# A mixture-of-experts stage on one core: second biases for all tokens at once, tokens gathered one expert ahead at set places, 15 instead of 17 ranks with split operands

## The chip, the cores and the metric

One Trainium2 chip, one of its cores. The metric is the device time of one launch in microseconds. TensorE (PE) multiplies into PSUM; VectorE (DVE), ScalarE (ACT) and GpSimd (POOL) do the rest; SyncE (SP) issues the weight transfers from DRAM.

## The reference

Three transformer blocks over 512 tokens of width 1024, in float32. The change touches the mixture of experts at the end of the first block:

```python
top_val, top_idx = lax.top_k(logits, TOP_K)          # 4 of 32 experts per token
gates = jax.nn.softmax(top_val, axis=-1)
u = xb @ w1[e] + b1[e]                               # 1024 -> 2048
glu = jnp.minimum(u[:, ::2], SWIGLU_LIMIT)
lin = jnp.clip(u[:, 1::2], -SWIGLU_LIMIT, SWIGLU_LIMIT)
a = glu * jax.nn.sigmoid(SWIGLU_ALPHA * glu) * (lin + 1.0)
y_e = a @ w2[e] + b2[e]                              # 1024 -> 1024
y = sum over the token's experts of gate * y_e
x = x + gt_f * y
```

Each expert has 12.6 MB of weights, and each is read once.

## The kernel before

The stage is `moe(k)` (line 951 on). A router ranks experts 1 to 31 by their number of tokens; expert 0 has rank 0 whatever its count. `ROOM` gives each rank its rows: 128, 96, 80 or 64. Tokens beyond a rank's room go to overflow blocks, which a loop at the end runs (none does here). Ranks 1 and 2 ("heavy") have a second block of 64 rows beside their 128.

An expert is three products ("gemms") of 8 contraction steps `kt` each, with 1024 output columns per step: two for the halves of the first layer, one for the second layer. A rank below `N1` ("large") runs on split operands: each weight unit of 128x1024 is copied rounded by ACT (`whi`, L302) and its remainder taken by DVE (`wlo`, L303), and each step is three products of two 512-column matmuls. A rank from `N1` up ("small", 64 rows) multiplies the raw float32 weights instead; the two column halves go to two halves of the array and no splitting is needed. Heavies do both.

Each gemm opens with a bias matmul (`bias` times a selector, L1306 for small, L1309 for large) and the weights follow (L1321). After either half of the first layer DVE and ACT form the gated activation (`gl`, L1338 to L1342), PE transposes it (`to_features`, L1252), and `put` (L1244, L1246) writes it as the operand `a`. After the third gemm ACT scales the rows by their gates (`yr`) and GpSimd adds them into a DRAM array by an indirect DMA (`scatter`). The tokens of an expert come by an indirect DMA from `hrow` (`gather`, L1275 for small, L1279 for large) into one of two tiles `xg`, are transposed and put as operand `x`.

The weights stream through a ring of nine 1 MB tiles `mraw` and two `raw`, issued by SP in one order. `Stream.ahead` starts splits up to three units ahead. The order of experts is written out by a planner: it alternates large and small by a budget and puts a heavy where the budget is low. With `N1 = 17` it gives 0, 3, 17, 4, 5, 18, 6, 7, 19, 8, 9, 20, 10, 11, 21, 12, 13, 22, 14, 15, 23, 16, 24, 1, 25, 26, 27, 2, 28, 29, 30, 31; with `N1 = 15` it gives 0, 3, 15, 4, 5, 16, 6, 7, 17, 8, 9, 18, 10, 11, 19, 12, 13, 20, 14, 21, 1, 22, 23, 24, 2, 25, 26, 27, 28, 29, 30, 31. The framework orders each engine's instructions by program order and by its own estimate of when their inputs are ready, within the edges it is given; `issue_after(ins)` is such an edge: instructions of the block stand behind `ins` on its engine. The tables of tokens and gates are formed during expert 0 (`tables`, `tables2`). For the last expert `collect()` takes two `mraw` tiles to read the DRAM sums back, and `first_weights` loads weights of the second block.

## Time and profile before

| | us |
|---|---|
| median of 3 runs | 3357.71 (3354.88 to 3361.1) |
| the profiled execution, its own time | 3355.98 |
| its span, first to last instruction | 3354.2 |
| busy PE / DVE / ACT / POOL in the span | 3210.9 / 1920.1 / 1337.2 / 411.0 |
| stage of the experts, first gemm of rank 0 to first gemm of rank 31 | 706.6 to 1819.6 |

Busy time of PE is the union of its matmuls, which overlap. In the trace a float32 matmul has two records. The stage's stretches are cut at the first bias matmul of each expert, which the timeline of PE shows. A profile row's last bracket names the idle time before an instruction and what ended it. In rows of stretches the columns are the stretch, its length, busy time (and number) on PE, PEld, DVE, ACT and POOL, the granted clock, the DMA engines' busy share and GB/s.

### The profile page before, as it was taken

Reading aid. Unit: us, or ns where it says so; the run is one execution under the profiler, and the core shown is the slowest. Engines: PE = TensorE matmul, PEld = TensorE weight load, DVE = VectorE, ACT = ScalarE, POOL = GpSimd, SP = SyncE. Lnnn points to the kernel's source line nnn. Section 1 sums busy time; section 2 is a strip of 40 time slices with the busy share of each in tenths; the row PEclk is TensorE's granted clock in tenths of the full one; section 3 lists DMA queues with packets and bytes.
Section 4 is the critical chain, followed back from the end, with each engine's and each line's share of the span. In section 5 each row is a group of like instructions: output and inputs, shape, how many; then the busy total and the mean of one; then the engine's idle time right before and its main releaser. Section 6 shows DMA issues by size and latency. Waiting matters only on the chain. (4 is left out here: it accounts for less than half of the span.)

```text
span 3354.2 us, 41112 instructions
## 1 busy us (share of the span) xinstructions
PE 3210.9 (96%) x15657; PEld 2236.1 (67%) x15657; DVE 1920.1 (57%) x2931; ACT 1337.2 (40%) x1972; POOL 411.0 (12%) x514
## 2 busy tenths in 40 slices
PE   6999999999999999999997899999999999999998
PEld 5778887776665555544342567777776777678876
DVE  7652235476786666844141477756547756555645
ACT  2233344345565555633131254322235433343433
POOL 1223000131000000000100100312120011110001
PEclk9999999999999999999999999999999999999999
DMA  7437313459999999996979312545332200022222
GB/s 268 170 119 237 111 71 115 184 200 354 393 393 380 378 374 371 378 387 239 407 298 367 139 59 75 191 155 187 132 116 75 98 25 3 30 85 96 93 91 85
DMA packets 110393, 664.75 MB, mean 198 GB/s; under 512 B 15452, under 2 KB 15556, under 8 KB 41712
## 3 DMA queue, kind: packets, MB, share of 16 engines
q1 hardware_dynamic: 81952, 573.35, 44.2%
q0 software_dynamic: 28240, 88.73, 8.9%
q8 instruction: 125, 2.05, 0.2%
q14 instruction: 76, 0.62, 0.1%
HBM read 647.04 MB, written 28.10 MB: 201 GB/s over the span
## 5 line engine op out<-in xcount | busy, mean ns | idle before, releaser
L302 ACT ACTIVATE whi<-raw 128x1024 fp32r<-128x1024 f32 x354 | 373.7, 1058 | 661.2 <-PE mm L353 512.3
L303 DVE TENSOR_TENSOR wlo<-raw,whi 128x1024 fp32r<-128x1024 f32 x352 | 434.5, 1238 | 311.7 <-ACT whi L302 304.9
L352 PE MATMUL mm<-h_hi,whi 128*128 128x512 f32 x1440 | 578.0, 401 | 4.7 <-DVE th L656 1.6
L353 PE MATMUL mm<-h_lo,whi 128*128 128x512 f32 x1440 | 577.5, 401 | 0.0
L354 PE MATMUL mm<-h_hi,wlo 128*128 128x512 f32 x1440 | 576.6, 400 | 0.0
L303 DVE TENSOR_TENSOR wlo<-mraw,whi 128x1024 fp32r<-128x1024 f32 x246 | 294.4, 1219 | 73.5 <-ACT whi L302 73.0
L352 PEld LDWEIGHTS mm<-h_hi,whi 128*128 128x128 f32 x1440 | 271.3, 188 | 83.0 <-issue 11.5
L353 PEld LDWEIGHTS mm<-h_lo,whi 128*128 128x128 f32 x1440 | 271.5, 189 | 68.2 <-issue 7.0
L354 PEld LDWEIGHTS mm<-h_hi,wlo 128*128 128x128 f32 x1440 | 271.5, 189 | 67.8 <-issue 5.6
L302 ACT ACTIVATE whi<-mraw 128x1024 fp32r<-128x1024 f32 x248 | 258.2, 1055 | 84.6 <-PE mm L1321 62.7
L1321 PE MATMUL s<-mraw,x 128*64 128x512 f32 x896 | 235.4, 605 | 23.9 <-DMA mraw<-in_w_dram 15.5
L1321 PE MATMUL mm<-whi,x 128*80 128x512 f32 (+2 forms) x816 | 242.4, 403 | 6.7 <-ACT whi L302 6.7
L1338 DVE TENSOR_SCALAR gl<-s 128x256 f32<-128x256 f32 x34 | 14.4, 423 | 309.4 <-PE s L1321 309.4
L1321 PEld LDWEIGHTS mm<-whi,x 128*80 128x80 f32 (+2 forms) x816 | 134.6, 168 | 76.2 <-issue 13.5
L1321 PEld LDWEIGHTS s<-mraw,x 128*64 128x64 f32 x896 | 65.7, 138 | 146.4 <-issue 123.3
L370 PE MATMUL mm<-whi,h_hi 128*128 128x256 f32 x480 | 138.3, 288 | 2.8 <-DVE rs L620 1.7
L352 PE MATMUL mm<-fhi,whi 128*128 128x512 f32 x352 | 139.2, 396 | 0.0
L353 PE MATMUL mm<-flo,whi 128*128 128x512 f32 x352 | 139.0, 395 | 0.0
L354 PE MATMUL mm<-fhi,wlo 128*128 128x512 f32 x352 | 138.9, 395 | 0.0
L1339 ACT ACTIVATE gt<-gl 128x256 f32<-128x256 f32 (+3 forms) x68 | 35.5, 522 | 257.7 <-DVE gl L1338 256.2
L371 PE MATMUL mm<-wlo,h_hi 128*128 128x256 f32 x480 | 136.4, 284 | 1.8 <-DVE wlo L303 1.7
L1321 PE MATMUL mm<-wlo,x 128*80 128x512 f32 (+2 forms) x408 | 131.7, 404 | 5.6 <-DVE wlo L303 4.3
(731 smaller groups left out, 5560.3 us busy)
## 6 DMA issues: line engine op xcount, KB each, us to landing
mraw<-in_w_dram SPq DMA_DIRECT2D x316, 1024.0 KB, 8.9
raw<-in_w_dram SPq DMA_DIRECT2D x68, 1024.0 KB, 9.7
mw<-in_wmod_dram POOLq DMA_DIRECT2D x48, 512.0 KB, 4.2
raw<-in_w_dn_dram SPq DMA_DIRECT2D x24, 1024.0 KB, 4.8
raw<-in_w_gu_dram SPq DMA_DIRECT2D x22, 1024.0 KB, 4.9
raw<-in_w_up_dram SPq DMA_DIRECT2D x22, 1024.0 KB, 4.8
mw<-in_wada_dram POOLq DMA_DIRECT2D x32, 512.0 KB, 4.4
raw<-in_w_aqk_dram SPq DMA_DIRECT2D x12, 1024.0 KB, 4.8
```

The lines of the kernel that those rows point to most:

```text
L302: nc.scalar.activation(hi, raw, AF.Copy)
L303: ins = (nc.gpsimd if pool_lo else nc.vector).tensor_sub(lo, raw, hi.bitcast(F32))
L352: nc.tensor.matmul(pss[t], hi[:, k, s], xs[0][:, k0 + k], start=first, stop=False)
L353: nc.tensor.matmul(pss[t], hi[:, k, s], xs[1][:, k0 + k], start=False, stop=False)
L354: nc.tensor.matmul(pss[t], lo[:, k, s], xs[0][:, k0 + k], start=False, stop=last)
L370: nc.tensor.matmul(ps, xs[0][:, k, s], hi[:, k % 4], start=k == 0, stop=False)
L371: nc.tensor.matmul(ps, xs[0][:, k, s], lo[:, k % 4], start=False, stop=False)
L1321: ins = nc.tensor.matmul(o[c], l(kt), r_[:, c * 512:(c + 1) * 512], start=False, stop=kt == 7 and n_ == len(terms) - 1)
L1338: V.tensor_scalar(gl, pg, 7.0, None, op0=ALU.min)
L1339: S.activation(th, gl, AF.Tanh, scale=0.5 * 1.702)
```

## The change

`N1` goes from 17 to 15, and `ROOM` gives ranks 15 and 16 64 rows. `gemm` leaves the bias matmul out of the third gemm. In its place `tables2` forms `gT`, the gate of each token for each expert (one product and one sum on DVE, a copy on ACT, four transposes, a copy on ACT), and `bias2(n)` adds, for eight feature tiles, second bias times `gT` to `x` (one float32 matmul of 512 columns, one DVE instruction); the eight are handed to rank 30 (`order[-2]`), two per step in the second half of its first gemm. `gather` returns its transposes as steps; `expert` gathers for the expert that follows it and places the steps with `issue_after` behind steps 3 and 5 of its second gemm, or behind steps 3 to 5 of the third when either is heavy, or behind 5 and 6 of the third in expert 0. The transposes of the activation are placed behind step 2 of the next gemm. `sw` (the selector) is copied by ACT, not GpSimd. The five units whose remainder GpSimd took in expert 0 (6, 10, 12, 14, 19) go to DVE.

```diff
--- before.py
+++ after.py
@@ -942,9 +942,9 @@
     k.wcol = None
 
 
-N1 = 17
+N1 = 15
 N2 = 2
-ROOM = (128,) * 6 + (96,) * 4 + (80,) * 7 + (64,) * 15
+ROOM = (128,) * 6 + (96,) * 4 + (80,) * 5 + (64,) * 17
 OV = 32 + N2
 NB = OV + 15
 
@@ -1181,6 +1181,16 @@
         V.tensor_copy(ovi, ov[0:1])
         V.tensor_tensor(sel[:, :, 32:47], ov[:, 1:16].unsqueeze(1).to_broadcast([128, 2, 15]),
                         pmod.unsqueeze(2).to_broadcast([128, 2, 15]), op=ALU.is_equal)
+
+        V.tensor_tensor(big.rearrange("p (t r) e -> p t r e", t=4), E, gate.unsqueeze(3).to_broadcast([128, 4, 4, 32]), op=ALU.mult)
+        gr = e2[:, 0:128].rearrange("p (t e) -> p t e", t=4)
+        V.tensor_reduce(gr, big.rearrange("p (t r) e -> p t e r", t=4), axis=AX.X, op=ALU.add)
+        g4 = e1[:, 512:1024].rearrange("p (t a e) -> p t a e", t=4, a=4)
+        S.activation(g4, gr.unsqueeze(2).to_broadcast([128, 4, 4, 32]), AF.Copy)
+        ps = k.pt("t")
+        for t in range(4):
+            nc.tensor.transpose(ps[:, t * 128:(t + 1) * 128], g4[:, t].rearrange("p a e -> p (a e)"), k.ident)
+        S.activation(gT, ps, AF.Copy)
         g = k.v("g_final")
         g2 = ep.tile([128, 8], F32, name="g2", bufs=1)
         V.tensor_mul(g2, g, g)
@@ -1189,6 +1199,7 @@
         pools["Y"] = es.enter_context(tc.tile_pool(name="Yp", bufs=1))
 
     pools = {}
+    gT = k.sm.tile([128, T], F32, tag="nwt", name="gT", bufs=1)
     nsp = [len(early)]
 
     def wsplit(raw, pool_lo=False, to=None):
@@ -1218,7 +1229,7 @@
                 if self.big[u] and u not in self.split:
                     if len(self.split) >= limit:
                         return
-                    self.split[u] = wsplit(self.raw(u), u in (6, 10, 12, 14, 19))
+                    self.split[u] = wsplit(self.raw(u))
 
         def take(self):
             u = self.at
@@ -1267,34 +1278,43 @@
 
     def gather(blocks):
 
-        X = []
+        X, steps = [], []
         for ns, gidx, *_ in blocks:
             xg = xgs[ng[0] % 2]
             ng[0] += 1
+            w, n = (128, 4) if ns == 64 else (ns, 8)
             if ns == 64:
                 G.indirect_dma_start(xg[:, 0:512], None, hrow2, IOA(ap=gidx, axis=0), bounds_check=2 * T - 1, oob_is_err=False)
-                hl, at = operand("x", False, lambda v, kt: v[:, kt % 4, 64 * (kt // 4):64 * (kt // 4) + 64])
-                to_features([v[:, 0:4] for v in hl], xg[:, 0:512], 4, 128)
             else:
                 G.indirect_dma_start(xg[0:ns], None, hrow, IOA(ap=gidx[0:ns], axis=0), bounds_check=T - 1, oob_is_err=False)
-                hl, at = operand("x", True, lambda v, kt, ns=ns: v[:, kt, 0:ns])
-                for c in range(2):
-                    to_features([v[:, 4 * c:4 * c + 4] for v in hl], xg[0:ns, 512 * c:512 * c + 512], 4, ns)
-            X.append(at)
-        return X
-
-    def expert(blocks, selcol, X=None, between=None, last=False):
-
-
-        X = X or gather(blocks)
+            hl = []
+
+            def step(c, hl=hl, ns=ns, n=n, w=w, xg=xg):
+                if not hl:
+                    hl += operand("x", ns > 64, (lambda v, kt: v[:, kt % 4, 64 * (kt // 4):64 * (kt // 4) + 64]) if ns == 64 else
+                                  (lambda v, kt: v[:, kt, 0:ns]))
+                to_features([v[:, 4 * c:4 * c + 4] for v in hl[0]], xg[0:w, 512 * c:512 * c + 512], 4, w)
+            X.append(lambda hl=hl: hl[1])
+            steps += [lambda c=c, step=step: step(c) for c in range(n // 4)]
+        return X, steps
+
+    def expert(blocks, selcol, X=None, between=None, last=False, after=None):
+
+
+        if X is None:
+            X, steps = gather(blocks)
+            for f in steps:
+                f()
+            X = [x() for x in X]
         A = [operand("a", False, lambda v, kt: v[:, kt // 4 * 2 + kt % 2, 64 * (kt % 4 // 2):64 * (kt % 4 // 2) + 64]) if b_[0] == 64
              else operand("a", True, lambda v, kt, ns=b_[0]: v[:, kt, 0:ns]) for b_ in blocks]
         split = any(b_[0] > 64 for b_ in blocks)
         if blocks[-1][0] == 64:
             sw = ep.tile([128, 128], F32R, tag="sw", name="sw")
-            G.tensor_copy(sw.rearrange("p (c s) -> p c s", c=2), selcol.to_broadcast([128, 2, 64]))
-
-        def gemm(ops, bcol):
+            S.activation(sw.rearrange("p (c s) -> p c s", c=2), selcol.to_broadcast([128, 2, 64]), AF.Copy)
+
+        def gemm(ops, bcol, hooks={}):
+
 
             pss = []
             with tc.issue_after(turn["mm_ins"]) if turn.get("mm_ins") else nullcontext():
@@ -1302,7 +1322,9 @@
                     ps = bank("s").unsqueeze(1) if ns == 64 else bank("mm", (128, 2, 512))
                     o = [ps[64 * c:64 * c + 64, 0] if ns == 64 else ps[0:ns, c] for c in range(2)]
                     b_ = bias[:, bcol // 2:bcol // 2 + 512]
-                    if ns == 64:
+                    if bcol == 2048:
+                        pass
+                    elif ns == 64:
                         nc.tensor.matmul(ps[:, 0], sw, b_, start=True, stop=False)
                     else:
                         for c in range(2):
@@ -1318,19 +1340,30 @@
                     terms = ((op_[0], hi), (op_[0], lo), (op_[1], hi)) if len(op_) == 2 else ((op_[0], raw),)
                     for n_, (l, r_) in enumerate(terms):
                         for c in range(2):
-                            ins = nc.tensor.matmul(o[c], l(kt), r_[:, c * 512:(c + 1) * 512], start=False,
+                            ins = nc.tensor.matmul(o[c], l(kt), r_[:, c * 512:(c + 1) * 512], start=bcol == 2048 and kt + n_ == 0,
                                                    stop=kt == 7 and n_ == len(terms) - 1)
                 if not looped:
                     stream.ahead(stream.at + (3 if split else 6))
                 turn["mm_ins"] = ins.ins
                 if kt == 3:
                     turn["half"] = ins.ins
+                for f in hooks.get(kt, ()):
+                    with tc.issue_after(ins.ins):
+                        f()
                 for _ in range(2 if kt > 3 else 0):
                     if adds:
                         adds.pop(0)()
             return [ps if b_[0] == 64 else ps[0:b_[0]] for (ps, _), b_ in zip(pss, blocks)]
+        heavy = len(blocks) > 1 or after and len(after) > 1
+        hooks, pend = {}, []
+        Xn = None
+        if after and not between:
+            Xn, steps = gather(after)
+            if not heavy:
+                hooks = {3 + 2 * i: [f] for i, f in enumerate(steps)}
         for hf in range(2):
-            for ps, (a_, _), (ns, *_) in zip(gemm(X, hf * 1024), A, blocks):
+            todo = []
+            for ps, (a_, _), (ns, *_) in zip(gemm(X, hf * 1024, {**hooks, 2: pend} if hf else {}), A, blocks):
                 w, nh = ps.shape[0:2]
                 pg, pl = ps[:, :, 0:256], ps[:, :, 256:512]
                 tl = lambda name, bufs: ep.tile([128, 2, 256], F32, tag=name, name=name, bufs=bufs)[0:w, 0:nh]
@@ -1341,12 +1374,19 @@
                 V.scalar_tensor_tensor(gl, th, 1.0, gl, op0=ALU.add, op1=ALU.mult)
                 V.scalar_tensor_tensor(gl, ln, 1.0, gl, op0=ALU.add, op1=ALU.mult)
                 n = 2 * nh
-                to_features([v[:, n * hf:n * hf + n] for v in a_], gl.rearrange("p a b -> p (a b)"), n, w, 0.5)
+                todo.append(lambda a_=a_, gl=gl, n=n, w=w, hf=hf: to_features([v[:, n * hf:n * hf + n] for v in a_], gl.rearrange("p a b -> p (a b)"), n, w, 0.5))
+            pend = todo
             if hf and between and not last:
                 between[1]()
+        hooks = {2: pend}
+        if after and between:
+            Xn, steps = gather(after)
+            hooks.update({5 + i: [f] for i, f in enumerate(steps)})
+        elif heavy and after:
+            hooks.update({3 + i: [f] for i, f in enumerate(steps)})
         adds.extend(collected)
         collected.clear()
-        pys = gemm([a_[1] for a_ in A], 2048)
+        pys = gemm([a_[1] for a_ in A], 2048, hooks)
         for py, (ns, _, tok, gcol, *row) in zip(pys, blocks):
             if not last:
                 scatter(py, gcol, row[0], ns)
@@ -1358,6 +1398,7 @@
             adds.pop(0)()
             if between and len(adds) == 0:
                 between()
+        return Xn and [x() for x in Xn]
 
     def block(b):
         return (ROOM + (64,) * N2)[b], tabi[:, b:b + 1], tab[:, 0, b:b + 1], tab[:, 1, b:b + 1], tabi[:, b:b + 1]
@@ -1373,7 +1414,6 @@
         order.append(kinds[kind].pop(0))
         ahead += {"small": -4, "large": 2, "heavy": 11}[kind]
     assert sorted(order) == list(range(32)) and order[-1] >= N1
-    k.sg = k.sm.tile([128, T], F32, tag="nwt", name="sg", bufs=1)
 
     yd, yd2 = k.yd, k.yd.rearrange("t (a b) -> (t a) b", a=2)
     collected = []
@@ -1471,15 +1511,23 @@
     stream.split.update(enumerate(early))
     with tc.issue_after(last.ins):
         stream.ahead(4, 4)
-    for p in order:
-        blocks = [block(p)] + ([block(31 + p)] if 1 <= p <= N2 else [])
-        if p == 0:
-            expert(blocks, sel[:, :, 0:1], pick(A0), (tables, tables2))
-            continue
+    def bias2(n):
+
+        r_ = slice(0, 64) if n < 4 else slice(64, 128)
+        ps = bank("mm", (128, 2, 512))[:, 0]
+        nc.tensor.matmul(ps, bias[r_, 1024 + 128 * (n % 4):1152 + 128 * (n % 4)].bitcast(F32), gT[r_], start=True, stop=True)
+        V.scalar_tensor_tensor(k.x[:, n], ps, mod[:, 40 + n:41 + n], k.x[:, n], op0=ALU.mult, op1=ALU.add)
+    Xc = pick(A0)
+    blocks = lambda p: [block(p)] + ([block(31 + p)] if 1 <= p <= N2 else [])
+    for i_, p in enumerate(order):
         own = p == order[-1]
+        if p == order[-2]:
+            adds.extend([lambda n=n: bias2(n) for n in range(8)])
         if own:
+            k.sg = k.sm.tile([128, T], F32, tag="nwt", name="sg", bufs=1)
             collected.extend(collect())
-        expert(blocks, sel[:, :, p:p + 1], last=own, between=first_weights if own else None)
+        Xc = expert(blocks(p), sel[:, :, p:p + 1], Xc, last=own, between=(tables, tables2) if p == 0 else first_weights if own else None,
+                   after=None if own else blocks(order[i_ + 1]))
     nov = nc.values_load(ovi[0:1, 0:1], min_val=0, max_val=15)
     with tc.For_i(0, nov, 1) as i:
         e = nc.values_load(ovi[0:1, bass.ds(i + 1, 1)], min_val=0, max_val=31)
```

## Rows read from the trace of the kernel before

**Rows 1.** The page: span, DMA in 40 slices, DVE's splits, weight transfers.

```profile
span 3354.2 us, 41112 instructions
...
DMA  7437313459999999996979312545332200022222
...
L303 DVE TENSOR_TENSOR wlo<-mraw,whi 128x1024 fp32r<-128x1024 f32 x246 | 294.4, 1219 | 73.5 <-ACT whi L302 73.0
...
mraw<-in_w_dram SPq DMA_DIRECT2D x316, 1024.0 KB, 8.9
```

**Rows 2.** Stretches by expert: ranks 17, 14, 15, 23, 16, 25, 26, 31.

```profile
801.45:826.52 25.07, 25.03 (x113) 8.34 (x111) 8.44 (x13) 7.62 (x11) 3.50 (x3) 1.00 0.94 360
1345.82:1385.96 40.14, 38.34 (x169) 23.99 (x167) 35.64 (x37) 29.06 (x33) 1.59 (x1) 0.96 0.97 383
1385.96:1422.17 36.21, 36.12 (x165) 23.02 (x164) 32.10 (x34) 25.19 (x28) 2.52 (x2) 1.00 0.97 367
1422.17:1450.66 28.49, 26.08 (x113) 8.46 (x112) 4.10 (x10) 3.96 (x8) 3.85 (x4) 1.00 0.97 376
1450.66:1489.02 38.36, 36.58 (x164) 22.93 (x163) 33.33 (x34) 26.60 (x29) 1.58 (x1) 1.00 1.01 406
1588.04:1614.03 25.99, 25.54 (x111) 8.32 (x109) 3.21 (x8) 2.78 (x7) 4.67 (x4) 1.00 1.00 357
1614.03:1641.51 27.48, 25.99 (x110) 8.23 (x108) 3.21 (x8) 3.07 (x7) 4.01 (x4) 1.00 1.02 417
1819.58:1862.48 42.90, 25.48 (x90) 7.44 (x88) 6.80 (x11) 5.23 (x8) 3.79 (x5) 0.84 0.96 387
```

**Rows 3.** Sum over the stretches of all small experts but the last, 14.

```profile
sum 385.46, PE 365.04 PEld 118.37 DVE 58.47 ACT 54.65 POOL 51.94; mean PE 26.07 PEld 8.46 DVE 4.18 ACT 3.90 POOL 3.71
```

**Rows 4.** Timeline of PE: start, us, what; a small expert and the next large.

```profile
1215.88 1.94 PE L1321 MATMUL s<-raw,x 128*64 128x512 f32 x8 [1.34 <-ACT x L1244]
...
1224.96 0.41 PE L1252 MATMUL t<-ident,gl 128*128 128x128 f32 x2 [0.56 <-DVE gl L1342]
...
1244.36 0.69 PE L1321 MATMUL mm<-whi,x 128*80 128x512 f32 x2 [1.11 <-ACT whi L302]
```

**Rows 5.** PE's waits in the stage: total us, times, longest.

```profile
PE t L1252 <- DVE gl L1342: 16.4, 22, 3.7
PE s L1321 <- ACT x L1244: 9.8, 10, 1.3
```

**Rows 6.** Timeline of PE: a large expert's third gemm and the transposes in it.

```profile
1201.67 0.62 PE L1309 MATMUL mm<-bias,sel 128*80 128x512 f32 x2
1202.12 0.63 PE L1321 MATMUL mm<-whi,a 128*80 128x512 f32 x2
...
1207.45 0.44 PE L1252 MATMUL t<-ident,gl 80*128 80x80 f32 x4
```

**Rows 7.** Timeline: GpSimd's remainder in expert 0, and DVE beside it.

```profile
718.74 3.05 POOL L303 TENSOR_TENSOR wlo<-raw,whi 128x1024 fp32r<-128x1024 f32 x1 [10.63 <-ACT whi L302]
719.42 2.41 DVE L1139 TENSOR_SCALAR ki<-ki 128x16 int32<-128x16 int32 x1
...
721.74 0.16 DVE L1140 TENSOR_SCALAR ki<-ki 128x16 int32<-128x16 int32 x1
...
749.47 1.85 DVE L1171 TENSOR_TENSOR tabi<-tf,pad 128x17 int32<-128x17 f32 x1
```

**Rows 8.** Timeline: SP and PE about the start of rank 31.

```profile
1807.83 10.48 SPq L296 DMA_DIRECT2D raw<-in_w_qk_dram  x2
...
1824.28 14.67 SPq L969 DMA_DIRECT2D mraw<-in_w_dram  x9
...
1832.11 6.46 PE L1321 MATMUL s<-mraw,x 128*64 128x512 f32 x16 [12.04 <-DMA mraw<-in_w_dram]
```

**Rows 9.** Landing of the gathers of tokens.

```profile
DMA to landing us min/median/max: 4.4/7.4/9.9
```

**Rows 10.** Landing of the scatters of results.

```profile
DMA to landing us min/median/max: 3.6/9.0/14.1
```

## The prediction

> **What bounds the kernel now.** I read the page first. Its DMA line is near full in slices 10 to 18 of 40, the stage of the experts, so weights could be the bound there [rows 1]. The stretches by expert say otherwise. In a second large expert of a pair PE is busy 36.12 of 36.21 us, in the first small expert 25.03 of 25.07, while DVE is at 32.10 of 36.21 or far below [rows 2]. The list of PE's waits has only short ones, on operands: 16.4 us on the activation `gl` in 22 places, 9.8 us on the gathered tokens `x` in 10 [rows 5]. So TensorE's in-order queue sets the pace, and weights flow as fast as tiles come free. A few stretches differ. A large expert behind a small one takes 40.14 or 38.36 us instead of 36.21, because the first splits come late (1.11 us on `whi` in one case) and the granted clock falls to a mean of 0.96 in the 40.14 [rows 2, 4]. Rank 31 waits 12.04 us for its first weights: SP stood 10.48 us before two transfers of the next block's weights and issued rank 31's only from 1824.28 on, though rank 31 began at 1819.58 [rows 2, 8].
>
> How near are the transfers? Ranks 14, 15 and 23 moved 40.14x383 + 36.21x367 + 28.49x376 = 39.4 MB in 104.84 us, 376 GB/s, with the DMA engines 0.97 busy; rank 26 shows 417 GB/s at a share of 1.02 [rows 2]. I take 417 as the ceiling: at 376 SP was still waiting for free tiles. Transfers are therefore a close second.
>
> **The change part by part**, against the profiled execution's own 3355.98 us (median 1.7 above).
>
> *Two ranks from split to raw.* Ranks 15 and 16 took 36.21 and 38.36 us, 74.6 together [rows 2]. By the reference's own inputs they hold 62 and 58 tokens, so 64 rows suffice and the overflow loop stays empty. What does a small expert take when nothing waits? 25.07 (rank 17) and 25.99 (rank 25) with three bias matmuls [rows 2]; one bias is 1202.12 - 1201.67 = 0.45 us [rows 6]. The mean less one bias is 25.1; I take 25.2. Two of them: 50.4. **-24.2.**
>
> *Set places for tokens and activation in small experts.* The 14 small experts before rank 31 take 385.5 us now [rows 3]. Their excess over 25.2 is the wait for `x` at the start (1.34), waits for `gl` in the later gemms (0.56 in one) [rows 4], and the bias. With tokens transposed in the expert before, and the activation's transposes behind step 2 of the next gemm (three steps of the eight, where the wait shows them taken about one step too early), these go. 385.5 - 14x25.2 = **-32.7.** Next is the transfers, below.
>
> *Biases off the large and heavy ones.* 0.45 x (12 large + rank 0) + 0.9 x 2 heavies = **-7.6.** DVE, at 32 to 36 us of work per large [rows 2], still fits in 35.8 and 39.7. Between 0 (DVE is the next bound) and -7.6 I take the full value, since in both large stretches it had 4 us to spare.
>
> *Expert 0.* Five remainders move from GpSimd to DVE: 5x1.22 = +6.1 us of DVE [rows 1]. But beside a GpSimd remainder a 16-element DVE instruction took 2.41 us where its neighbour took 0.16, and a 17-element one 1.85 [rows 7]: each such meeting cost DVE about 2 us, so five may give back 10. `gT` adds two 512-element passes, half the 1.22 each, 1.2 us in all. Net -3 on DVE; between +7 (nothing given back) and -5, I take **-2** on PE.
> The Trainium skill, "SBUF — State Buffer", section "Who interferes with whom", says that GpSimd and a DVE instruction on their shared port exclude each other for a whole instruction. The rows agree in kind. By that rule the gain could reach the whole time of the GpSimd instructions, some 3 us each by the one in rows 7, and the sum would be about 5 us lower.
>
> *Transfers for 17 small experts.* This is what eats the gain. A small expert needs 12x1.05 MB [rows 1] plus an estimated 0.5 MB of gathered and scattered rows, 13.1 MB: 31.4 us at 417 GB/s against 25.2 of PE. It lives on the ring: 11 tiles, 11.5 MB, less what is in flight (8.9 us to landing [rows 1], 3.7 MB), so 7.8 MB. In the mixed part a period of two large and one small falls from 104.84 to about 39.7 + 35.8 + 25.2 = 100.7 us and needs 391 GB/s, under 417: no wait. Three smalls between the heavies need (39.3 - 7.8)/0.417 = 75.5 us, PE wants 75.6: no wait. After the second heavy there are now six smalls before rank 31, not three: (78.6 - 7.8)/0.417 = 169.8 against 151.2: **+18.6.**
>
> *Second biases at once.* Eight float32 matmuls of 512 columns. In rows 4 eight records of a small expert start within 1.94 us; a bias is two records, so 0.4 to 0.9 us, 3.5 to 7 in all. They stand in rank 30, where PE by then waits some 6 us for weights; without that cover they cost the 7. `gT`'s transposes stand in expert 0. I take **+1** for both.
>
> *Rank 31* loses one bias, **-0.4.** Its late loads stay: `collect()` takes its two tiles in front of them as before.
>
> *Moved queues.* The gather on POOL now stands in front of the scatter of the same expert and behind that of the one before; GpSimd is idle most of the time (3.85 busy of 28.49 us [rows 2]). The selector's copy on ACT falls into smalls, where ACT is busy 3.96 of 28.49 [rows 2]: nothing.
>
> Sum: -24.2 - 32.7 - 7.6 - 2 + 18.6 + 1 - 0.4 = -47.3. 3355.98 - 47.3 = **3309 us.**
>
> **The rivals.**
> *Better (3291):* the set places also clear the late splits at the six small-to-large boundaries, 40.14 or 38.36 down towards 36.2, about 3 us each: -18. For: the tokens' puts leave ACT and DVE at the boundary. Against: ACT there waits in line behind the scatter's copy, which the change leaves.
> *Set places too early in large experts (3337):* `gl` is ready 5.3 us after the first weight matmul of the third gemm [rows 6], some 23 matmuls; behind step 2 are 18, 4.2 us. If the transposes stand right there PE waits 1.2 us in the third gemm and 0.7 in the second, where a bias still covers: 1.9 x 15 = +28. Against: the edge sets the earliest place only.
> *Transfers bound throughout (3360, no change):* if 376 GB/s is already all that the mixed part can move, each of six periods stays at 104.84 (+4.1 each, +25), the last six smalls need 188.3 instead of 169.8 (+18.5), the three between the heavies 83.8 (+8): 3309 + 51. For: a share of 0.97. Against: 406 and 417 in other stretches [rows 2].
> The Trainium skill, "DMA: Bandwidth & Descriptors", section "Where 436 GB/s comes from", goes further and sets about 358 GB/s per core from HBM. Then a period would take 110 us, the tail another 28 and the middle 12, and the sum would be an estimated 3405. The rows with 383 to 417 speak against it; I give it 1 in 100, within this rival.
> *Gathers late at a hard place (slower, 3396):* a small expert's step stands about 12 us after the expert's start (a gemm of 8.4 and half the next). A gather lands in 7.4, at most 9.9 us [rows 9]. Were it held until the scatter issued ahead of it had landed, 9.0 us [rows 10], it would land near 17 and hold PE's whole queue 5 us in each of 17 smalls: +87. It decides from 2.8 us of lateness per small, that is landing 14.8 us after the start. Against: both kinds already run next to each other, and no gather took over 9.9.
>
> **How the numbers follow.** Forecast 0.54, better 0.12, early places 0.16, transfers throughout 0.10, late gathers 0.08. Likeliest: 3309. Terms at their ends (expert 0 from -5 to +7, bias gain 0, ring 2 MB more or less at 417 GB/s, so 5 us) make 3295 to 3330 around it; with the better case and the early places the range is 3286 to 3344, which leaves out 0.18. A measurement of this kernel can tell 0.2%, 6.7 us. Faster by more: 0.54 + 0.12 + 0.16 = 0.82; within: 0.10; slower: 0.08.
>
> **What would show it.** Small experts of about 25.2 us in the first part, no waits on `x`, no third-gemm bias; pairs of large ones at 35.8 for the second; the first large of a pair still 38 to 40. In the six smalls before rank 31, waits of PE on weights, and stretches near 31 us at a DMA share of 1. Rank 31 starting near 1772 and still waiting about 12 us. Wrong would be: waits on `gl` in large experts, waits on `x` longer than before, no waits on weights in the tail, or a tail that begins earlier than its third small.

## The result and the profile after

| kernel | median us (range) | ratio to before, 95% interval | profiled span us |
|---|---|---|---|
| before | 3357.24 (3350.81 to 3364.30) | 1 | 3354.2 |
| changed | 3314.69 (3311.63 to 3319.82) | 0.9873 [0.9862, 0.9885] | 3314.7 |

3309 was predicted, 3286 to 3344 as the range. The time lies 5.7 us above the forecast. Errors of up to 12 us in both directions lie behind that and cancel in part, as the stretches show. First the page of the changed kernel (the answer to [rows 1]): the span, the DMA share and GB/s in 40 slices, and the landing of weights.

```profile
span 3314.7 us, 40635 instructions
...
DMA  7537423378999999979899213545332300122222
GB/s 267 177 110 216 135 80 106 134 243 326 388 399 396 385 381 380 412 270 415 320 416 395 75 45 117 178 141 201 118 118 67 111 13 3 39 80 99 89 97 82
...
mraw<-in_w_dram SPq DMA_DIRECT2D x316, 1024.0 KB, 12.4
```

The 17th, 19th and 21st slices now stand at 412 to 416 GB/s, and a weight tile lands 12.4 us after its issue instead of 8.9 [rows 1]. Next, stretches by expert, as in [rows 2]: time, then the busy time of PE, PE's weight loads, DVE, ACT and GpSimd, the granted clock, the DMA share and GB/s. They are expert 0, ranks 10, 11 and 19 (large, large, small), rank 23, ranks 26 and 29 of the last six small ones, and the start of rank 31. The clock is a share of the higher of its two levels, 2.4 GHz, so 0.50 is 1.2 GHz.

```profile
712.52:765.59 53.07, 48.37 (x252) 40.11 (x250) 51.71 (x111) 30.90 (x39) 3.14 (x3) 0.97 0.78 267
1132.45:1173.49 41.04, 38.13 (x167) 23.54 (x166) 36.63 (x38) 29.47 (x33) 3.35 (x2) 0.96 1.02 405
1173.49:1210.30 36.81, 36.01 (x162) 22.65 (x160) 30.84 (x32) 25.27 (x28) 2.43 (x2) 1.00 1.00 387
1210.30:1234.15 23.85, 23.85 (x111) 7.61 (x109) 4.20 (x10) 3.78 (x8) 2.50 (x2) 1.00 0.93 363
1490.81:1514.35 23.54, 23.54 (x108) 7.63 (x106) 3.21 (x8) 3.09 (x7) 2.64 (x2) 1.00 1.02 416
1636.87:1669.05 32.18, 32.18 (x124) 9.80 (x122) 8.93 (x16) 3.08 (x7) 2.64 (x2) 1.00 1.02 416
1720.44:1750.89 30.45, 25.65 (x108) 7.00 (x107) 3.21 (x8) 3.08 (x7) 1.58 (x1) 1.00 1.02 417
1781.33:1822.00 40.67, 22.23 (x86) 5.72 (x84) 6.80 (x11) 4.85 (x7) 3.77 (x5) 0.83 0.95 383
```

A small expert takes 23.5 to 23.9 us with PE never idle; in the tail it takes 30.45, with PE busy 25.65 and the DMA engines full. A large expert is longer than before: rank 11 takes 36.81, and took 36.21. Three sums of stretches say the same of all of them: the 14 small experts of ranks 17 to 30 after ([rows 3] has them before), the 12 large ones (ranks 3 to 14) before, and the same 12 after.

```profile
sum 366.98, PE 349.91 PEld 107.93 DVE 57.52 ACT 48.94 POOL 39.35; mean PE 24.99 PEld 7.71 DVE 4.11 ACT 3.50 POOL 2.81
```

```profile
sum 456.80, PE 445.13 PEld 307.11 DVE 404.28 ACT 326.23 POOL 28.71; mean PE 37.09 PEld 25.59 DVE 33.69 ACT 27.19 POOL 2.39
```

```profile
sum 463.66, PE 442.38 PEld 302.00 DVE 401.25 ACT 326.28 POOL 35.74; mean PE 36.86 PEld 25.17 DVE 33.44 ACT 27.19 POOL 2.98
```

In the large ones PE has 2.75 us less to do (445.13 to 442.38) and is idle 9.6 us more (456.80 - 445.13 = 11.67 before, 463.66 - 442.38 = 21.28 after). What it waits for in the stage (total us, times, longest; [rows 5] before):

```profile
PE s L1343 <- DMA mraw<-in_w_dram: 30.7, 28, 11.8
PE mm L1343 <- ACT whi L302: 5.5, 5, 1.1
PE mm L1343 <- ACT a L1255: 5.1, 12, 0.8
PE t L1192 <- ACT h L1189: 4.2, 1, 4.2
PE mm L1343 <- DVE a L1257: 3.5, 10, 0.4
...
PE t L1263 <- DVE gl L1375: 2.0, 4, 1.0
```

The wait for `x` is gone, that for `gl` is 2.0 us instead of 16.4, and there are 8.6 us of waits for `a`, the operand of the third gemm, in 22 places. A first source of them stands in the timeline of PE about the third gemm of rank 11 (start, us, what; in brackets the idle time ahead and its releaser):

```profile
1190.85 0.44 PE L1263 MATMUL t<-ident,gl 80*128 80x80 f32 x4
1191.36 0.60 PE L1263 MATMUL t<-ident,xg 128*128 128x128 f32 x4
...
1203.10 0.44 PE L1263 MATMUL t<-ident,gl 80*128 80x80 f32 x4
1203.33 0.44 PE L1343 MATMUL mm<-ws,a 128*80 128x512 f32 x1
1204.07 0.69 PE L1343 MATMUL mm<-whi,a 128*80 128x512 f32 x2 [0.29 <-ACT a L1255]
...
1205.61 1.15 PE L1343 MATMUL mm<-whi,a 128*80 128x512 f32 x4 [0.39 <-DVE a L1257]
```

Before, the transposes of the next tokens (`xg`) stood right behind those of `gl` in the third gemm (0.5 us after the row at 1207.45 in [rows 6]):

```profile
1207.97 0.49 PE L1252 MATMUL t<-ident,xg 128*128 128x128 f32 x3
```

Now they stand in the second, at 1191.36, and behind 1203.33 PE has nothing that doesn't need `a`. A second source, on DVE, shows in e12 below.

### The profile page after: what moved, and what is told of

It reads as the page before. It is cut to its first block, busy times and chain, and to the rows that moved or that the text cites. A ratio compares the mean times of both kernels' runs of the same rounds, so it can differ in the third digit from the quotient of the medians.

```text
span 3314.7 us, 40635 instructions
## 1 busy us (share of the span) xinstructions
PE 3167.1 (96%) x15510; PEld 2192.7 (66%) x15510; DVE 1861.5 (56%) x2890; ACT 1294.5 (39%) x1943; POOL 390.6 (12%) x492
## 5 line engine op out<-in xcount | busy, mean ns | idle before, releaser
L302 ACT ACTIVATE whi<-raw 128x1024 fp32r<-128x1024 f32 x343 | 362.1, 1058 | 665.2 <-PE mm L353 519.3
L303 DVE TENSOR_TENSOR wlo<-raw,whi 128x1024 fp32r<-128x1024 f32 x343 | 423.6, 1238 | 320.9 <-ACT whi L302 314.4
L303 DVE TENSOR_TENSOR wlo<-mraw,whi 128x1024 fp32r<-128x1024 f32 x223 | 267.6, 1219 | 81.0 <-ACT whi L302 80.0
L1343 PE MATMUL s<-mraw,x 128*64 128x512 f32 x1008 | 247.1, 607 | 27.2 <-DMA mraw<-in_w_dram 25.7
L302 ACT ACTIVATE whi<-mraw 128x1024 fp32r<-128x1024 f32 x223 | 232.1, 1055 | 87.4 <-PE mm L1343 68.7
L1343 PE MATMUL mm<-whi,x 128*128 128x512 f32 (+2 forms) x720 | 215.7, 404 | 5.5 <-ACT whi L302 5.5
L1343 PEld LDWEIGHTS mm<-whi,x 128*128 128x128 f32 (+2 forms) x720 | 119.1, 170 | 65.5 <-issue 14.9
L372 PE MATMUL mm<-whi,h_lo 128*128 128x256 f32 x480 | 137.5, 287 | 0.0
L1343 PE MATMUL s<-mraw,a 128*64 128x512 f32 x504 | 122.6, 602 | 6.3 <-DMA mraw<-in_w_dram 5.1
## 6 DMA issues: line engine op xcount, KB each, us to landing
mraw<-in_w_dram SPq DMA_DIRECT2D x316, 1024.0 KB, 12.4
```

What stands on the lines that cost most here:

```text
L302: nc.scalar.activation(hi, raw, AF.Copy)
L303: ins = (nc.gpsimd if pool_lo else nc.vector).tensor_sub(lo, raw, hi.bitcast(F32))
L372: nc.tensor.matmul(ps, xs[1][:, k, s], hi[:, k % 4], start=False, stop=k == 7)
L1343: ins = nc.tensor.matmul(o[c], l(kt), r_[:, c * 512:(c + 1) * 512], start=bcol == 2048 and kt + n_ == 0, stop=kt == 7 and n_ == len(terms) ...
```

## The experiments

Rank 0 to rank 31 is called the stage: 1113.02 us before (706.56 to 1819.58), 1068.81 in the changed kernel (712.52 to 1781.33). Stretches are cut at each expert's first bias matmul.

| run | median us | ratio to before, 95% interval | stage us | 12 large us | 16 small us | from rank 31 on us |
|---|---|---|---|---|---|---|
| changed | 3314.7 | 0.9873 [0.9862, 0.9885] | 1068.8 | 463.7 | 417.0 | 1533.4 |
| e1_x_third | 3302.1 | 0.9823 [0.9810, 0.9837] | 1056.7 | 452.0 | 416.5 | 1535.2 |
| e2_pool | 3320.6 | 0.9881 [0.9865, 0.9897] | 1076.3 | 463.8 | 416.6 | 1534.2 |
| e3_n17 | 3326.3 | 0.9897 [0.9881, 0.9912] | 1083.0 | (14) 541.5 | (14) 351.7 | 1534.7 |
| e4_bias3 | 3316.6 | 0.9886 [0.9862, 0.9911] | 1071.5 | 463.8 | 420.0 | 1532.5 |
| e5_gt_late | 3309.6 | 0.9851 [0.9836, 0.9866] | 1069.9 | 463.7 | 417.3 | 1536.3 |
| e8_order | 3305.7 | 0.9840 [0.9825, 0.9855] | 1062.2 | 464.4 | 408.0 | 1535.2 |
| e9_collect_late | 3305.3 | 0.9835 [0.9820, 0.9850] | 1068.7 | 463.6 | 416.8 | 1530.0 |
| e10_all | 3293.3 | 0.9808 [0.9794, 0.9821] | 1061.3 | 453.4 | 418.0 | 1522.9 |
| e11_x_now | 3302.3 | 0.9831 [0.9815, 0.9848] | 1056.6 | 452.6 | 415.4 | 1538.4 |
| e12_gl_now | 3330.8 | 0.9920 [0.9903, 0.9936] | 1088.6 | 457.1 | 439.3 | 1536.3 |
| e13_best | 3293.8 | 0.9807 [0.9793, 0.9822] | 1060.7 | 451.9 | 419.8 | 1525.2 |

What is missing between the columns lies in expert 0 and in the heavy ones. Expert 0 takes 53.1 to 54.8 us in runs that don't touch it (e1, e3, e8, e9).

The granted clock moves the column of the large ones too. In rank 10 of the changed kernel it is 0.50 from 1136 to 1139 us, behind waits of 1.11 and 0.57 us for the first split, and the first gemm takes 15.33 us; behind the same waits in e1 it stays at 1.00 and the gemm takes 13.76. Such a fall, in an expert that follows a small one, comes in three of the 12 before, in the changed kernel and in e4 and in two in e1, e11 and e12, at other ranks from profile to profile; why there stays open. So 1.6 us of what e1, e11 and e12 gain in the large ones is the clock's.

**e1_x_third, e11_x_now: where the next tokens' transposes stand.** The first puts them into the third gemm of a large expert:

```diff
-            if not heavy:
+            if not heavy and not split:
                 hooks = {3 + 2 * i: [f] for i, f in enumerate(steps)}
...
-        elif heavy and after:
+        elif (heavy or split) and after:
             hooks.update({3 + i: [f] for i, f in enumerate(steps)})
```

> The changed kernel, but a large expert puts the next expert's token transposes behind steps 3 and 4 of its third gemm instead of steps 3 and 5 of its second; small ones as in the change. Theory (the trace after shows PE waiting 0.29 to 0.55 us for the operand a or for DVE at the start of a large expert's third gemm, where before the next tokens' transposes lay over that time): the 12 large experts fall from 463.7 us by 0.5 to 1 us each, 6 to 10 us in all, to about 3306 us; the third gemm of a pair's second large expert falls from 12.9 to about 12.4 us plus the transposes. Rival (the large ones are longer because DVE or ACT has more to do, or because splits come late): the waits only change place and the time stays within 2 us of 3314.7.

Measured: the large ones fall by 11.7 us, the stage by 12.1. PE in the same place of rank 11:

```profile
1192.68 0.44 PE L1263 MATMUL t<-ident,gl 80*128 80x80 f32 x4
1192.92 0.44 PE L1343 MATMUL mm<-ws,a 128*80 128x512 f32 x1
1193.20 0.60 PE L1263 MATMUL t<-ident,xg 128*128 128x128 f32 x4
1193.65 0.69 PE L1343 MATMUL mm<-whi,a 128*80 128x512 f32 x2
...
1195.20 1.15 PE L1343 MATMUL mm<-whi,a 128*80 128x512 f32 x4 [0.39 <-DVE a L1257]
```

The 0.29 us wait is gone, and some 0.45 us of transposes (1193.20 to 1193.65) take no time of their own. The nine large experts whose clock is the same in both fall by 0.81 us each (7.27 in all), so some 10 of the 11.7 are the edit's. The theory holds, with its rival in part: the wait for `a` on DVE is still there.

The second takes the set place away for all experts:

```diff
-                   after=None if own else blocks(order[i_ + 1]))
+                   after=None)
```

> The changed kernel, but every expert's tokens are gathered and transposed in the program at its own start, as before the change, with no set place for the transposes; all else as changed. Theory (the set place one expert ahead is worth the 1.3 us wait for x at the start of a small expert, but costs a large expert the cover over its wait for a, some 1 us): the ten or so small experts that wait for no weights grow by 1 to 1.5 us each, the 12 large ones shrink by about 1 us each, the stage stays within 6 us of 1068.8 and the whole within 8 of 3314.7. Rival (the set place is worth its gain in every expert): small and large ones both longer, the stage by 15 to 25 us.

Measured: large ones 11.1 us shorter, as said, but the small ones 1.6 shorter too, not longer. With nothing set, `xg` stands here (PE, the end of the large rank 11, then the small rank 19 that follows it):

```profile
1188.01 0.49 PE L1263 MATMUL t<-ident,xg 128*128 128x128 f32 x3
...
1205.20 0.44 PE L1263 MATMUL t<-ident,gl 128*128 128x128 f32 x2
...
1212.58 0.44 PE L1263 MATMUL t<-ident,gl 128*128 128x128 f32 x2
1212.95 1.08 PE L1343 MATMUL s<-mraw,a 128*64 128x512 f32 x4
1213.96 0.77 PE L1263 MATMUL t<-ident,xg 80*128 80x80 f32 x8
```

They are still taken ahead of the expert that they are for, in the third gemm of the one before, behind `gl`. So the set place of the tokens gains nothing in a small expert and costs a large one some 0.8 us, the clock's part left out.

**e12_gl_now: the activation's transposes without a set place.**

```diff
-                todo.append(lambda a_=a_, gl=gl, n=n, w=w, hf=hf: to_features([v[:, n * hf:n * hf + n] for v in a_], gl.rearrange("p a b -> p (a b)"), n, w, 0.5))
+                to_features([v[:, n * hf:n * hf + n] for v in a_], gl.rearrange("p a b -> p (a b)"), n, w, 0.5)
```

> The changed kernel, but the activation's transposes have no set place behind step 2 of the next product; they stand in the program right behind the activation, as before the change. Theory (PE waited 16.4 us for gl in 22 places before, 2.0 us in the changed kernel): the waits for gl come back, small experts without a wait for weights grow by 0.5 to 1.1 us each, large ones by 0 to 0.5, the stage by 8 to 14 us. Rival (the waits for gl fell because the tokens' transposes left that place, not because of the set place): the stage within 3 us of 1068.8, waits for gl still near 2 us.

Measured: the stage 19.8 us longer, the small ones 22.3, the heavy ones 2.5 (137.52 for 135.07); the large ones 6.6 shorter. More than either expected. The waits of PE in the stage, and the timeline of the small rank 19:

```profile
PE t L1263 <- DVE gl L1375: 22.2, 26, 1.9
...
PE s L1343 <- DMA mraw<-in_w_dram: 18.1, 8, 12.4
```

```profile
1216.90 1.07 PE L1343 MATMUL s<-raw,x 128*64 128x512 f32 x2
1218.68 0.41 PE L1263 MATMUL t<-ident,gl 128*128 128x128 f32 x2 [0.71 <-DVE gl L1375]
...
1227.09 1.02 PE L1343 MATMUL s<-mraw,a 128*64 128x512 f32 x2
1229.31 0.41 PE L1263 MATMUL t<-ident,gl 128*128 128x128 f32 x2 [1.20 <-DVE gl L1375]
```

The same place in the changed kernel:

```profile
1218.07 1.94 PE L1343 MATMUL s<-raw,x 128*64 128x512 f32 x8
1219.84 1.03 PE L1343 MATMUL s<-mraw,x 128*64 128x512 f32 x4
1220.80 0.44 PE L1263 MATMUL t<-ident,gl 128*128 128x128 f32 x2
```

Without the set place the transposes stand behind two records of matmuls instead of twelve. From 1216.90 two records take 1.78 us up to the transposes, as long as eight take from 1218.07. The rank takes 27.54 us instead of 23.85, 3.7 more; only 1.9 of these are listed as waits, since a matmul's modelled end counts part of the gap as busy. Of the two set places it is this one that gains in the small experts. The waits for weights fall (18.1 from 30.7), as small experts that take longer ask for them less fast.

In the large experts the same set place costs time. Ranks 7, 9, 11 and 13, at a granted clock of 1.00 in both, are 0.55 to 0.64 us shorter without it. DVE's part of `a` in rank 11's third gemm, in the changed kernel and then in this run:

```profile
1202.80 2.35 DVE L303 TENSOR_TENSOR wlo<-mraw,whi 128x1024 fp32r<-128x1024 f32 x2
1205.07 0.48 DVE L1257 SCALAR_TENSOR_TENSOR a<-t,a 128x320 fp32r<-128x320 f32 x1
```

```profile
1202.25 1.22 DVE L303 TENSOR_TENSOR wlo<-mraw,whi 128x1024 fp32r<-128x1024 f32 x1
1203.50 0.49 DVE L1257 SCALAR_TENSOR_TENSOR a<-t,a 128x320 fp32r<-128x320 f32 x1
```

With the set place two remainders stand ahead of it in DVE's queue, and without, as before the change, one. The 0.39 us wait of PE for DVE's `a` (at 1205.61 above) is in rank 11 of the changed kernel and of e1 and not of e12. A run with this set place in the small experts alone was not made.

**e2_pool: GpSimd takes five remainders of expert 0 again.**

```diff
-                    self.split[u] = wsplit(self.raw(u))
+                    self.split[u] = wsplit(self.raw(u), u in (6, 10, 12, 14, 19))
```

> The changed kernel, but GpSimd takes the remainders of five of expert 0's weight tiles again. Theory (the GpSimd remainders shut DVE out, which gave back more than the 2 us forecast): expert 0 grows from 53.1 us to about 58 to 61 us and the whole by 5 to 8 us, to about 3320 to 3323. Rival (the five remainders on DVE cost as much as they give back; expert 0 is shorter for another reason, the order of its transposes): no change within 1 us, or 2 to 6 us faster.

Measured: expert 0 takes 60.81 us, 7.7 more. The stretch, GpSimd's remainders, and DVE's last step of the activation beside one (733.21) and beside none (757.75):

```profile
709.50:770.31 60.81, 52.29 (x251) 42.37 (x250) 55.21 (x106) 30.61 (x38) 19.41 (x8) 0.88 0.70 239
```

```profile
721.78 3.06 POOL L303 TENSOR_TENSOR wlo<-raw,whi 128x1024 fp32r<-128x1024 f32 x1 [15.29 <-ACT whi L302]
727.42 8.07 POOL L303 TENSOR_TENSOR wlo<-mraw,whi 128x1024 fp32r<-128x1024 f32 x2 [2.57 <-ACT whi L302]
```

```profile
733.21 2.83 DVE L1374 SCALAR_TENSOR_TENSOR gl<-gt,gl 128x512 f32<-128x512 f32 x1
...
757.75 0.68 DVE L1374 SCALAR_TENSOR_TENSOR gl<-gt,gl 128x512 f32<-128x512 f32 x1
```

DVE is busy 55.21 us with five splits fewer, 51.71 with them: they cost 6.1 us of DVE and give back 9.6. One of the instructions held up is `gl`, on PE's path: PE waits 5.6 us for it in this run, and 0.3 us or less for any step of DVE in the changed kernel's expert 0. In all it waits 8.5 us and not 4.7, 3.8 more. The other 3.9 of the 7.7 are PE's busy time (52.29 for 48.37): while PE stands idle ahead of `gl` the granted clock falls to 0.50, and it stays there until some 745 us. The theory holds.

**e3_n17: 17 experts on split operands.**

```diff
-N1 = 15
+N1 = 17
...
-ROOM = (128,) * 6 + (96,) * 4 + (80,) * 5 + (64,) * 17
+ROOM = (128,) * 6 + (96,) * 4 + (80,) * 7 + (64,) * 15
```

> The changed kernel, but with 17 experts on split operands again (ranks 15 and 16 have room for 80 tokens). Theory (a small expert saves PE 12 to 13 us against a large one but needs its weights in less time, so part of it comes back as waits for weights further on): the two ranks take about 24.5 us more, the waits of PE on weights in small experts (30.7 us in all) fall by 12 to 20, net +5 to +12, 3320 to 3327 us. Rival (the two ranks are worth their whole 24.5 us): about 3339 us, waits on weights unchanged.

Measured: 11.6 us more in the whole, 14.2 in the stage, as the theory has it. The two ranks are 36.79 and 40.57 us long (the second at a mean clock of 0.96), 27.3 more than 26.07 and 23.96; the waits of PE for weights are 20.7 us instead of 30.7, and the 14 small experts that stay small are 15.3 us shorter (351.7 for 367.0).

**e4_bias3: the second bias in the third gemm again**, in every expert, without `gT` and the eight matmuls at once.

```diff
-                    if bcol == 2048:
-                        pass
-                    elif ns == 64:
+                    if ns == 64:
...
-        if p == order[-2]:
-            adds.extend([lambda n=n: bias2(n) for n in range(8)])
```

> The changed kernel, but every expert adds its second bias in its third gemm again (one matmul in a small one, two in a large one), and neither the gate sums by expert, their transposes nor the eight matmuls at once are there. Theory (a bias matmul is 0.45 us of PE; in the large experts it lay over the wait for the operand a, so taking it out gave nothing there): large experts unchanged within 0.3 us each, small ones ahead of the tail +0.4 each, expert 0 about 4 us shorter because the 4.2 us wait for the transposed gate sums goes; the whole within 4 us of 3314.7. Rival (every bias taken off is worth its 0.45 us, as forecast): 13 to 15 us slower than the changed kernel less the 4 us, about 3325.

Measured: 3316.6 us; large ones unchanged within 0.1 us in all, small ones 0.57 us longer each where no weights are awaited, expert 0 1.8 shorter. The theory holds but for expert 0's 4.

**e5_gt_late: `gT`'s transposes behind expert 0's last product.**

```diff
-        ps = k.pt("t")
-        for t in range(4):
-            nc.tensor.transpose(ps[:, t * 128:(t + 1) * 128], g4[:, t].rearrange("p a e -> p (a e)"), k.ident)
-        S.activation(gT, ps, AF.Copy)
+        def turned():
...
+        late.append(turned)
...
+            hooks[7] = list(late)
```

> The changed kernel, but the transposes of expert 0's gate sums stand behind step 7 of expert 0's third gemm instead of right behind the tables, with the copy they wait for in a tile of its own. Theory (they stand ahead of everything else in TensorE's queue and it waits 4.2 us there for ScalarE's copy): expert 0 falls from 53.1 to about 49 us, the whole by 4 us. Rival (what stands behind them is not ready either, or ScalarE and VectorE set expert 0's pace): expert 0 within 1 us of 53.1, another wait in its place.

Measured: expert 0 takes 53.70 us, no less. The 4.2 us wait is replaced by one for `ov` (1.9) and one for a split of DVE (2.2): the rival. The median is 5 us lower; in the two profiles the difference lies ahead of the stage (below).

**e8_order, e9_collect_late, e10_all, e13_best: can the waits for weights be moved away?**

```diff
+    order = [0, 3, 4, 15, 16, 5, 6, 17, 18, 7, 8, 19, 20, 1, 21, 22, 9, 10, 23, 24, 11, 12, 25, 26, 13, 14, 27, 28, 2, 29, 30, 31]
     assert sorted(order) == list(range(32)) and order[-1] >= N1
```

> The changed kernel, but with another order of the experts: two large, two small in turn and the two heavy ones in the middle and third from the end, so that no more than two small ones follow each other. Theory (waits for weights are a matter of how many small experts stand in a row: the ring of weight tiles empties, by about 7.7 us of transfer for each small one): small experts lose some 12 us to weights instead of 34, the last stretch before rank 31 no more than 4, the whole 15 to 25 us shorter than 3314.7. Rival (transfers bound the stage throughout, at some 385 GB/s over it): the same loss in other places, within 5 us of 3314.7.

Measured: the stage 6.6 us shorter, between the two. In five of the seven pairs the second small one now takes 27.2 to 28.4 us. Ranks 5, 6, 17 and 18 together in this run, and in the run that has the shorter large ones as well (e10_all):

```profile
889.31:1019.68 130.37, 123.83 (x543) 69.77 (x541) 76.15 (x88) 62.57 (x76) 10.30 (x8) 0.99 1.02 404
```

```profile
884.41:1014.51 130.10, 122.53 (x543) 68.52 (x541) 75.86 (x88) 62.30 (x76) 11.22 (x8) 1.00 1.02 405
```

The large ones in it are 3.4 us shorter (75.41 for 78.77), the small ones 3.1 longer (54.69 for 51.60): the sum stays, with the transfers at 404 to 405 GB/s and a share of 1.02 in both.

```diff
-        adds.extend(collected)
-        collected.clear()
+        if last and not looped:
+            adds.extend(collect())
...
-            collected.extend(collect())
```

> The changed kernel, but the collecting step's two weight tiles are taken only ahead of rank 31's third gemm, so that rank 31's own first loads no longer stand behind them. Theory: the wait of 11.8 us for weights at rank 31's start goes, the whole falls by 8 to 12 us. Rival (after six small experts the ring is empty anyway and rank 31's weights could not land earlier): rank 31 still waits 7 us or more, or the wait moves behind rank 31 to the collecting step; within 4 us of 3314.7.

Measured: the profile gives 3.5 us from rank 31 on and nothing in the stage. The 11.8 us wait is gone, but smaller ones stand in its place, 11.2 us in all in rank 31's three gemms: the rival's 7 us or more. The longest, 5.72, is ahead of the third gemm, where the collecting tiles now stand; whether they or the empty ring cause it is not separated. The median is 9 us lower, with single runs from 3300.6 to 3315.0; what is beyond the 3.5 I don't claim.

> The changed kernel with four edits together: large experts' token transposes in the third gemm (that run alone gave 3302), the gate sums' transposes late, the other order of experts, the collecting step's tiles late. Theory (they shorten different places): about 12 + 4 + 20 + 10 us under 3314.7, 3265 to 3280 us. Rival (with fewer waits on operands the transfers bind throughout, by 406 MB of weights and rows over the stage at no more than 417 GB/s): 3285 to 3300 us.

Measured: 3293.3 us, the rival's number. Rank 31 finds its weights landed (10.5 us less from there on), but the stage is longer than with the first edit alone (1061.3 against 1056.7).

For the last run the experts' order is the change's up to its end, and a heavy expert stands shortly ahead of rank 31 (with the edits of e1 and e9):

```diff
+    order = [0, 3, 15, 4, 5, 16, 6, 7, 17, 8, 9, 18, 10, 11, 19, 12, 13, 20, 14, 21, 22, 23, 1, 24, 25, 26, 27, 28, 2, 29, 30, 31]
```

> The changed kernel with three edits: large experts' token transposes in the third gemm (3302 alone), the collecting step's tiles late (3.5 us less from rank 31 on, alone), and the experts' order of the change except for its end: 14, 21, 22, 23, 1, 24 to 28, 2, 29, 30, 31, so that the second heavy expert fills the ring of weight tiles shortly ahead of rank 31. Theory: from rank 31 on as in the run with four edits (1522.9 us), the stage near the 1056.7 us of the first of these edits alone, 3284 to 3293 us. Rival (moving the heavy expert back only moves the waits for weights ahead of it, as transfers fill 0.97 of the stage): 3293 to 3300 us.

Measured: 3293.8 us, on the border of the two. From rank 31 on it gains 10.0 us over the first edit alone, and the stage gives 4.0 back, 3.3 of it in the small experts. Both this and e10_all beat the changed kernel by 21 us.

## Why the prediction was right, and where it was not

Against 3355.98, as the prediction counted, by stretches of the profiles:

| term | predicted us | measured us |
|---|---|---|
| ranks 15 and 16 | -24.2 | 74.57 to 50.02: -24.5 |
| 14 small experts, with the waits of the tail | -32.7 + 18.6 = -14.1 | 385.46 to 366.98: -18.5 |
| 12 large experts (their share of the biases) | -5.4 | 456.80 to 463.66: +6.9 |
| two heavy ones | -1.8 | 138.93 to 135.07: -3.9 |
| expert 0 (with its bias) | -2.4 | 57.26 to 53.07: -4.2 |
| rank 31 and what follows | -0.4 | -1.2 |
| second biases at once | +1 | in the rows above |
| ahead of the stage | 0 | 706.56 to 712.52: +6.0 |
| sum | -47.3 | -39.4 (the spans: -39.5) |

By the profiles the sum is 7.9 us off: 18.3 too little gained in the large experts and ahead of the stage, 10.4 more than forecast elsewhere. That these cancel so far is luck.

**The two ranks** were right to 0.3 us. What eats into them was there too: undone (e3), they cost 14.2 us in the stage and not the 27.3 that they are longer by.

**The small experts** gained 4.4 us more than forecast, and their cause was half right. Undisturbed they take 23.5 to 23.9 us where 25.2 was the floor, since the floor was read from stretches that still held a loss by `gl`'s transposes (25.07 and 25.99 [rows 2]; 25.22 in e12, which has that loss and no third bias). The prediction gave the two set places the credit together. Of them only `gl`'s earned it (e12: +22.3 us without it; e11: -1.6 us without the tokens'); the bias adds 0.57 us each (e4). **The heavy ones** have a block of 64 rows too, and the prediction gave them the bias alone: 1.35 of their 3.9 us are the bias's (e4: 136.42) and 2.45 the set place's (e12: 137.52).

**The failed step is "Biases off the large and heavy ones"**, in its sentence that DVE having 4 us to spare makes 0.45 us per bias sure in the large ones. Beside it, what both set places cost there stands in the sum at nothing. The 12 were to lose 5.4 us and grew by 6.9, with the same number of falls of the clock. With the bias back (e4) they stay at 463.8: beside an uncovered wait the bias is worth nothing. With the tokens' transposes back (e1) they take 452.0, with `gl`'s set place away (e12) 457.1, either with one fall of the clock less. Rank 11 is at a clock of 1.00 in all four profiles (us, from the second bias matmul to the first with `a`, and from there to the next expert; the third gemm before from its bias matmul):

| rank 11 | second gemm | third gemm |
|---|---|---|
| before | 12.20 | 12.39, bias and `xg` in it |
| changed | 12.30, `xg` in it | 12.94 |
| e1_x_third | 11.85 | 12.56, `xg` in it |
| e12_gl_now | 12.30, `xg` in it | 12.31 |

The tokens' transposes had lain over the wait for `a` in the third gemm; the change put them into the second, where they take 0.45 us of their own (12.30 for 11.85). `gl`'s set place lets a second remainder in ahead of DVE's part of `a`. DVE had time to spare in the mean, and yet PE waits for it, for what stands ahead in its queue. Even in e1 the third gemm without a bias is not shorter than the one before with it: of the 4.8 us that e1's large ones are under those before, one fall of the clock is 1.6, and in rank 11 the rest lies in the second gemm (12.20 to 11.85), for a reason that stays open. So no run shows that a bias less gains a large expert 0.45 us. The step should have asked what the transposes hide where they stand and what hides them where they go.

**Expert 0** gained more than the -2. The term for DVE was right in size (6.1 us taken on and about 10 given back were forecast, 6.1 and 9.6 measured); PE gained 7.7 us, since one of the instructions that GpSimd held up was `gl`, for which PE waited 5.6, and the granted clock fell behind that wait. The gate sums gave part of it back: without them (e4) expert 0 is 1.8 us shorter with one bias more, so they cost an estimated 2.2 us, near the spread of expert 0 over the runs, and a later place for them doesn't help (e5). The Trainium skill, "SBUF — State Buffer", section "Who interferes with whom", has the two exclude each other for a whole instruction, and the prediction read from it that the whole time of the GpSimd instructions could come back. The traces agree that one instruction is held for another (2.83 us against 0.68), but of some 16 us of remainders DVE got back 9.6.

**Transfers in the tail** came as forecast: ranks 25 to 30 take 168.0 us against 169.8, with 415 to 417 GB/s in ranks 26 to 29. They were to take 151.2 without waits and would now take 141, but where transfers set the time that error of the floor doesn't show. No expert in these runs moved over 418 GB/s, so the 417 held as a ceiling. Between the heavy ones no wait was forecast (75.5 us of transfers, 75.6 of PE): with the lower floor the three there want some 72 us of PE (the third, ahead of a heavy one, 24.9 as rank 21), the third waits 4.4 us for weights and takes 31.46, and they take 78.5 together. The Trainium skill, "DMA: Bandwidth & Descriptors", section "Where 436 GB/s comes from", puts the limit from HBM at some 358 GB/s per core, a stack's bandwidth shared by two. With one core at work the tail ran at 416 and the middle at 404, so that limit doesn't bind here.

**The second biases at once** cost nothing, for the reason given but not in the place given. They stand in rank 26, not 30 (PE's group in 1636.87 to 1669.05: line, operation, records, busy us and mean ns; the idle time before it):

```profile
L1518 PE MATMUL mm<-gT,bias 64*128 64x512 f32 x16 | 8.4, 628 | 0.0
```

Rank 26 takes 32.18 us where rank 25 takes 23.53, 8.65 more or 1.08 for each of the eight, above the bound of 0.9. That was read from the small experts' matmuls, float32 as well, but two of them stand in the two halves of the array: their records last as long (592 ns, the biases' 589) and start closer together. Without the eight (e4) the last six take 167.9 us, the same.

**Ahead of the stage** nothing was edited, and yet the changed kernel's profile reaches rank 0 6.0 us later. That is no effect of the change that these runs could show: the 13 profiles reach it at 703.6 to 714.5 us, three of those with `gT` (e5, e12, e13) at 703.6 to 706.1. One difference is a weight load of the modulation between 188 and 222 us that lands 7.0 us after its issue in the changed kernel, with DVE idle 1.9 us for it, and 5.0 at most in e12, with no such wait. Why the time differs from profile to profile stays open; it is the reason to compare stages, not only medians, where a run differs by under 6 us.

**The rivals.** Late splits at the boundary of small and large didn't go: 41.04 us for the first of a pair, and 5.5 us of waits on `whi` in five places. Places too early didn't show in the form forecast: `gl` is awaited 2.0 us in four places, not 1.9 in each of 15; what `gl`'s place costs the large ones (e12) goes by DVE's queue. The rival of transfers throughout lost in the changed kernel, but it is what probably stands next: in e1, with the large ones repaired, the stage is 1056.7 us, and no other order tried here came under it. Late gathers didn't show: no wait on `x`.

## What to carry to other kernels

Before moving a filler in an in-order queue to an earlier place, look at what waits directly behind its old place: the filler may be the cover of that wait, and a shorter list of waits elsewhere will not show the loss. An engine with time to spare in the mean can still be waited for: look at what stands ahead in its queue. Test two set places one by one, and by kind of stretch: here one gained 22 us in the small experts and lost some 5 in the large, and the other lost some 10. When a kernel's transfers fill 0.96 of a stage, cutting the compute of one stretch pays only until the ring of tiles is empty, and a new order moved more of the waits than it removed.

## What the runs showed of the hardware that was not expected

- The eight second biases, float32 with 64 rows and 512 columns, take 0.54 us per record (8.65 us for 16), where the small experts' weight records, also float32 of 512 columns but in the two halves of the array, take 0.22 (eight in 1.77 us), both at a granted clock of 1.00. That the halves are the reason is not shown by a run of its own.
- A GpSimd remainder over 128x1024 takes 2.4 to 4.0 us, where DVE takes 1.22, and two in a row (8.07 us) stretch a DVE instruction of 0.68 us to 2.83.
- The granted clock over expert 0 is 0.88 in e2, where PE is idle 8.5 of 60.81 us, and 0.97 in the changed kernel, idle 4.7 of 53.07. In e2 it is 0.50 from 735 to 745 us, from the wait of 5.56 us for `gl` on; in rank 10 of the changed kernel 0.50 for 3 us, which makes a gemm of 13.76 us take 15.33.
